# A two-block transformer on one core: the key bias traced into the first feed-forward product with loads on GpSimd's queue, position terms into the first attention, two modulation sums into the second attention

## The chip, the core and the metric

One NeuronCore of a Trainium2 chip runs the whole program. Its engines are TensorE (PE in the profile; PEld is its weight load), VectorE (DVE), ScalarE (ACT), GpSimd (POOL) and SyncE (SP, which only issues transfers here). Each works through its own instructions in order and waits for the others on semaphores. The metric is device time in microseconds, lower is better.

## The reference, cut to what matters

Two transformer blocks follow one another on x of shape 1 x 256 x 1024. The first has sparse attention with a gated MLP beside it and a SwiGLU network; the second is modulated by six rows computed from a vector c, and mixes latent attention with a state-space scan. The change touches the modulation and the position bias of the second block:

```python
mod = (jax.nn.silu(c) @ ada_w + ada_b)[:, None, :]
shift_m, scale_m, gate_m, shift_f, scale_f, gate_f = jnp.split(mod, 6, axis=-1)
...
h = rmsnorm(x, pre_norm_mix) * (1.0 + scale_m) + shift_m
proj = h @ w_in                                # q_lat, kv_lat, k_idx, w_idx, z, ...
...
bias = rel_bias[t5_bucket_2(pos_sel - pos_b[..., None])]
logits = jnp.einsum('bqhc,bqkc->bhqk', q_b, kv_sel) * scale + jnp.transpose(bias, (0, 3, 1, 2))
...
h2 = rmsnorm(x, pre_norm_ffn) * (1.0 + scale_f) + shift_f
```

`ada_w` is 1024 x 6144; row j of the modulation is columns j*1024 to (j+1)*1024 (0 shift_m, 1 scale_m, 2 gate_m, 3 shift_f, 4 scale_f, 5 gate_f). Rows 1 and 0 are needed at the end of the first block, 2 after the second block's mixer, 4 and 3 after that, 5 last.

## The kernel before

**Products.** The 256 tokens are two tiles of 128 (t0, t1). Each product is exact to fp32 by three matmuls: a weight tile `raw` of 512 KB is loaded by SP (`wload`, a ring of NRAW = 6 buffers), ACT casts it to `hi` (L266), DVE subtracts to `lo` (L267; a ring of four of each), and PE multiplies hi, lo and hi again with the two parts of the input (L274 to 276, columns up to 512; L351 to 353 with 256). So a load, a cast, a subtraction and twelve or more matmuls follow each other for every tile, and DVE's place in its own queue decides when PE gets a `lo`.

**Stages.** In the profiled execution: the first attention to about 127 us, its output product w_out to 150, the first feed-forward network (f1) to 362, of which the product with w_down is 280 to 362; then the latent projection `lat` (496 columns), `zproj` (the first four pairs of columns of z) and the key bias, to 435; the second attention to 570, its output product w_o_attn to 583; then the state-space part, its output products and the second feed-forward network to the end. `weave` interleaves generators by shares when it traces; after that a scheduler orders each engine by the order of tracing as priority and by its own model of when things are ready.

**Modulation sums.** `ada(j)` (L497 on) loads eight tiles `araw` of 512 KB on SP's queue, each multiplied by a column of silu(c) and added up on DVE (L504 for the first, L506 for seven), sums over partitions by four small matmuls (L518) and writes row j to DRAM. Its `araw` ring has two buffers of its own. The sums 1, 0, 2, 4, 3 are woven into f1, sum 5 into the second feed-forward network.

**Position terms and key bias.** `pos_prep` (L864 to L903, with loads on ACT's queue) turns the positions into clipped distances `rel_dr` in DRAM, and cuts the bias table into bf16 parts; it is traced at the start of f1, so its operations stand in w_out and f1. `key_bias` (L906 on) makes the bias of all 16 heads for 256 x 256 pairs. In eight steps it loads a tile `rb` of 512 KB from `rel_dr` (L914, SP's queue, two buffers; the source is four rows of keys, each spread over 32 partitions), clips it to the limits of the partition's bucket into `oh` (L917, one buffer), compares (L918, `is_equal`, back into rb), and then twice runs a burst of 24 small matmuls (L924) with an ACT copy into `kb` (L926). After every fourth step two tiles kb of 1 MB go to DRAM (L929); the second attention reads them as `bq`. Two steps' loads are placed by the scheduler in f1, the rest stands around `lat`: eight parts of the key bias are traced ahead of the first token tile of `lat`, two ahead of the second (KBN).

Of the kernel before, what the change touches and what calls it, by code (L numbers as in the profile page):

```python
# [20 lines left out]
P = 128  # L21
# [16 lines left out]
# how far one product runs ahead of its neighbour, and the shares in which interleaved parts are traced  # L38
KBN = (8, 2)
# [6 lines left out]
SCHED = {"a1": (2.0, 1.08), "f1": (3.0, 2.4), "f1ada": (1, 0, 2, 4, 3), "a2": (2.0, 0.63), "f2": (3.0, 1.45),  # L46
# [43 lines left out]
def body(tc, I, O):  # L90
# [91 lines left out]
    # ---------------------------------------------------------------- inputs that come first  # L182
# [27 lines left out]
    # ---------------------------------------------------------------- helpers  # L210
# [15 lines left out]
    def rstd2(a, b, n, eps):  # L226
        """(sum of squares + n*eps)**-0.5: the reciprocal norm over sqrt(n)"""
# [58 lines left out]
    def proj(W, c0, n, KT, xT, evac, extra=None, sizes=(2,), bank=ma, pre=None):  # L286
        """token-major product with columns c0..c0+n; evac(t, psum)"""
# [27 lines left out]
    def proj2(W, KT, xT, evac, order=None, sizes=(2,), tail=4):  # L315
        """token-major product with 1024 columns; xT(k) or a pair gives the stationary tiles"""
# [18 lines left out]
    def projT(W, c0, n, KT, xT, evac, bank=None, wide=True):  # L335
        """feature-major product; evac(first 128-column tile, psum of two tiles)"""
# [21 lines left out]
    def residual(t, accs, prow32, grow, shift, xT, want_r):  # L358
        """x += norm(mix) * gain, then the next norm's transposed input; its scale is left out when want_r"""
# [125 lines left out]
    # ---------------------------------------------------------------- modulation rows of the second block  # L485
# [12 lines left out]
    def ada(j, pl, bufs=2):  # L498
        acc = T(per, [P, 1024], tag="ada", bufs=1)
        for k in range(8):  # L500
            raw = wload(ktile(I["ada_w_2"], k, 1, j * D, D), (1, 1024), tag="araw", bufs=bufs, pl=pl)[:, 0]
# [29 lines left out]
    # ---------------------------------------------------------------- first block  # L531
# [17 lines left out]
    def first_rstd(t):  # L549
# [5 lines left out]
        r1[t] = rr  # L555

    with pool("a1") as ap, pool("a1w") as aw:
# [272 lines left out]
        with queued():  # L830
# [5 lines left out]
            conditioning()  # L836
            ck = compress(0, I["cmp_pos_k"][0], I["cmp_w1_k"][0], I["cmp_w2_k"][0])
# [586 lines left out]
```

## Time and profile before

| | us |
|---|---|
| three runs | 1040.60, 1036.82, 1041.38 |
| their median | 1040.6 |
| span of the profiled execution | 1032.4 |
| PE busy in it | 943.0 (91%) |
| DVE busy in it | 734.4 (71%) |
| ACT busy in it | 508.2 (49%) |

The profile is one execution on the chip. Its span runs from the first to the last instruction; a run's time has a few microseconds more around that. A page gives busy times and the chain of work that ended last; the other views used are a table of stretches, the waits of an engine, the chain piece by piece, and the instructions of one tile or line.

### The profile page before, as it was taken

Reading aid. Unit: us, or ns where it says so; the run is one execution under the profiler, and the core shown is the slowest. Engines: PE = TensorE matmul, PEld = TensorE weight load, DVE = VectorE, ACT = ScalarE, POOL = GpSimd, SP = SyncE. Lnnn points to the kernel's source line nnn. Section 1 sums busy time; section 2 is a strip of 40 time slices with the busy share of each in tenths; the row PEclk is TensorE's granted clock in tenths of the full one; section 3 lists DMA queues with packets and bytes.
Section 4 is the critical chain, followed back from the end, with each engine's and each line's share of the span. In section 5 each row is a group of like instructions: output and inputs, shape, how many; then the busy total and the mean of one; then the engine's idle time right before and its main releaser. Section 6 shows DMA issues by size and latency. Waiting matters only on the chain.

```text
span 1032.4 us, 15890 instructions
## 1 busy us (share of the span) xinstructions
PE 943.0 (91%) x6029; PEld 797.7 (77%) x6029; DVE 734.4 (71%) x1317; ACT 508.2 (49%) x873; POOL 20.5 (2%) x38
## 2 busy tenths in 40 slices
PE   7989999799999876799999949999999979999997
PEld 5766667589988655787786738889967859999885
DVE  6648788588887664489987546988897676565544
ACT  5427554334444342376576415876764454444442
POOL 1000000000000001000000000000000000000000
PEclk9999999989999988899999978999999989999999
DMA  8871358887888846666643359959666626666651
GB/s 285 256 268 42 123 183 263 247 268 231 295 289 305 268 118 191 187 175 175 192 129 97 123 153 237 225 136 229 159 192 206 204 84 203 192 191 219 185 184 41
DMA packets 158640, 200.02 MB, mean 194 GB/s; under 512 B 15564, under 2 KB 120293, under 8 KB 158565
## 3 DMA queue, kind: packets, MB, share of 16 engines
q1 hardware_dynamic: 137696, 184.61, 59.3%
q10 hardware_dynamic: 20868, 14.41, 4.7%
q8 instruction: 47, 0.77, 0.3%
q14 instruction: 29, 0.23, 0.1%
HBM read 193.45 MB, written 5.54 MB: 193 GB/s over the span
## 4 chain that ended last, share of the span: by engine, by line
PE 59%; DMA 19%; DVE 14%; issue 3%; ACT 3%; POOL 1%; SPq 0%; ACTq 0%; DVEq 0%; POOLq 0%
PE ma L275 6%; PE ma L274 6%; PE ma L276 6%; DVE lo L267 4%; PE ma L353 4%; DMA rb<-t 4%; PE ma L351 4%; PE ma L352 4%; PE mb L351 4%; PE mb L352 3%; PE mb L353 3%; PE mb L276 3%; PE mb L274 3%; PE mb L275 3%; DMA araw<-in_ada_w_dram 3%
## 5 line engine op out<-in xcount | busy, mean ns | idle before, releaser
L266 ACT CAST hi<-raw 128x1024 fp32r<-128x1024 f32 (+2 forms) x266 | 275.4, 1042 | 235.9 <-PE mb L276 79.5
L267 DVE TENSOR_TENSOR lo<-raw,hi 128x1024 fp32r<-128x1024 f32 (+2 forms) x266 | 319.9, 1212 | 90.7 <-ACT hi L266 88.8
L353 PE MATMUL ma<-xTh,lo 128*128 128x256 f32 x512 | 147.3, 288 | 0.9 <-DVE lo L267 0.8
L351 PE MATMUL ma<-xTh,hi 128*128 128x256 f32 x512 | 147.3, 288 | 0.0
L352 PE MATMUL ma<-xTl,hi 128*128 128x256 f32 x512 | 147.0, 287 | 0.0
L353 PE MATMUL mb<-xTh,lo 128*128 128x256 f32 x384 | 108.0, 281 | 0.5 <-DVE lo L267 0.5
L351 PE MATMUL mb<-xTh,hi 128*128 128x256 f32 x384 | 108.0, 281 | 0.0
L352 PE MATMUL mb<-xTl,hi 128*128 128x256 f32 x384 | 107.8, 281 | 0.0
L353 PEld LDWEIGHTS ma<-xTh,lo 128*128 128x128 f32 x512 | 98.7, 193 | 3.8 <-DVE lo L267 1.9
L351 PEld LDWEIGHTS ma<-xTh,hi 128*128 128x128 f32 x512 | 98.7, 193 | 1.2 <-issue 0.7
L352 PEld LDWEIGHTS ma<-xTl,hi 128*128 128x128 f32 x512 | 98.6, 193 | 1.1 <-issue 0.8
L274 PE MATMUL ma<-hi,xTh 128*128 128x512 f32 (+2 forms) x208 | 86.9, 419 | 12.8 <-ACT row L970 12.6
L275 PE MATMUL ma<-lo,xTh 128*128 128x512 f32 (+2 forms) x208 | 85.7, 414 | 7.1 <-DVE lo L267 7.1
L276 PE MATMUL ma<-hi,xTl 128*128 128x512 f32 (+2 forms) x208 | 84.5, 409 | 0.1
L353 PEld LDWEIGHTS mb<-xTh,lo 128*128 128x128 f32 x384 | 72.3, 188 | 1.3 <-DVE lo L267 0.7
L351 PEld LDWEIGHTS mb<-xTh,hi 128*128 128x128 f32 x384 | 72.3, 188 | 0.4 <-issue 0.4
L352 PEld LDWEIGHTS mb<-xTl,hi 128*128 128x128 f32 x384 | 72.3, 188 | 0.2 <-issue 0.2
L506 DVE SCALAR_TENSOR_TENSOR ada<-araw,t,ada 128x1024 f32<-128x1024 f32 x42 | 53.8, 1281 | 22.3 <-DMA araw<-in_ada_w_dram 22.1
L274 PEld LDWEIGHTS ma<-hi,xTh 128*128 128x128 f32 x208 | 41.7, 201 | 24.5 <-ACT row L970 13.0
L275 PEld LDWEIGHTS ma<-lo,xTh 128*128 128x128 f32 x208 | 41.6, 200 | 18.8 <-DVE lo L267 10.0
L276 PEld LDWEIGHTS ma<-hi,xTl 128*128 128x128 f32 x208 | 41.5, 199 | 9.5 <-issue 0.9
L275 PE MATMUL ma<-lo,hTh 128*128 128x512 f32 x88 | 35.0, 398 | 3.2 <-DVE lo L267 3.2
(411 smaller groups left out, 1769.4 us busy)
## 6 DMA issues: line engine op xcount, KB each, us to landing
raw<-in_w_in_dram SPq DMA_DIRECT2D x80, 512.0 KB
araw<-in_ada_w_dram SPq DMA_DIRECT2D x48, 512.0 KB
raw<-in_w_gate_up_dram SPq DMA_DIRECT2D x44, 512.0 KB
raw<-in_w_ffn_in_dram SPq DMA_DIRECT2D x44, 512.0 KB
raw<-in_w_down_dram SPq DMA_DIRECT2D x22, 512.0 KB
raw<-in_w_ffn_out_dram SPq DMA_DIRECT2D x22, 512.0 KB
raw<-in_w_out_dram SPq DMA_DIRECT2D x16, 512.0 KB
raw<-in_w_o_ssd_dram SPq DMA_DIRECT2D x16, 512.0 KB
```

The costliest lines, as they stand in the source:

```text
L266: s.copy(hi, raw)
L267: v.tensor_tensor(lo, raw, hi.bitcast(F32), op=OP.subtract)
L274: pe.matmul(out, xh, wh, start=start, stop=False)
L275: pe.matmul(out, xh, wl, start=False, stop=False)
L276: pe.matmul(out, xl, wh, start=False, stop=stop)
L351: pe.matmul(out, hi[:, k % pc, fs], xh[:, k], start=k == 0, stop=False)
L352: pe.matmul(out, hi[:, k % pc, fs], xl[:, k], start=False, stop=False)
L353: pe.matmul(out, lo[:, k % pc, fs], xh[:, k], start=False, stop=k == KT - 1)
L506: v.scalar_tensor_tensor(acc, raw, cc, acc, op0=OP.mult, op1=OP.add)
```

## The change

`pos_prep` and its tiles move from the start of f1 into the first attention, behind `conditioning()`. `key_bias` is traced inside f1, between the modulation sums 0 and 2, and its loads go to GpSimd's queue (`g.dma_start`) instead of SP's. `lat` then runs alone. The sums 4 and 3 leave f1 and are woven into the second attention, with a share of 0.4 of the second part's; there they use the common `raw` ring of six instead of a ring of their own. Comments and docstrings are also taken out, which shifts line numbers: L267 becomes L266, the rb load L914 becomes L615, its clip and comparison L618 and L619, the bursts L625.

```diff
-SCHED = {"a1": (2.0, 1.08), "f1": (3.0, 2.4), "f1ada": (1, 0, 2, 4, 3), "a2": (2.0, 0.63), "f2": (3.0, 1.45),
+SCHED = {"a1": (2.0, 1.08), "f1": (3.0, 2.4), "a2": (2.0, 0.63), "f2": (3.0, 1.45),
...
-    def ada(j, pl, bufs=2):
+    def ada(j, pl=None):
         acc = T(per, [P, 1024], tag="ada", bufs=1)
+        own = dict(tag="araw", bufs=2, pl=pl) if pl else {}
         for k in range(8):
-            raw = wload(ktile(I["ada_w_2"], k, 1, j * D, D), (1, 1024), tag="araw", bufs=bufs, pl=pl)[:, 0]
+            raw = wload(ktile(I["ada_w_2"], k, 1, j * D, D), (1, 1024), **own)[:, 0]
...
+    ppg = pool("pp", side="right")
+    pp = ppg.__enter__()
...
-                sy.dma_start(rb, bass.AP(tensor=rd.tensor, offset=rd.offset + (k * P + kk * 4) * S,
-                                         ap=[[8 * S, 4], [0, 32], [1, 8 * S]]))
+                g.dma_start(rb, bass.AP(tensor=rd.tensor, offset=rd.offset + (k * P + kk * 4) * S,
+                                        ap=[[8 * S, 4], [0, 32], [1, 8 * S]]))
...
             conditioning()
+            pos_prep()
...
-    pos_prep()
     wa, wd = SCHED["f1"]
     weave((ffn(xT, I["w_gate_up"][0], I["w_down"][0], rf, ev_f1), wa),
-          (seq(*(ada(j, rp) for j in SCHED["f1ada"])), wd))
+          (seq(ada(1, rp), ada(0, rp), key_bias(), ada(2, rp)), wd))
+    rpg.__exit__(None, None, None)
+    ppg.__exit__(None, None, None)
...
-    lat = proj(W, 0, 496, 8, xT, ev_lat, extra=[(0, 0, 464), (464, 6608, 32)], sizes=(4,))
-    for n in KBN:
-        steps_of(kbg, n)
-        steps_of(lat, 1)
-    run(lat)
-    run(kbg)
-    rpg.__exit__(None, None, None)
+    run(proj(W, 0, 496, 8, xT, ev_lat, extra=[(0, 0, 464), (464, 6608, 32)], sizes=(4,)))
...
-    weave((seq(indexer(), latent_v(), heads()), wa), (seq(zproj(NZ0, NZ - NZ0), *gproj, ssd_in(0, ap)), wf))
+    weave((seq(indexer(), latent_v(), heads()), wa), (seq(zproj(NZ0, NZ - NZ0), *gproj, ssd_in(0, ap)), wf),
+          (seq(ada(4), ada(3)), wf * 0.4))
```

How the scheduled order changes is shown at three places of DVE's queue. The numbers in names are buffers and differ between the kernels.

The end of w_out in the kernel before (`lo` are its last four splits, `pi` parts of the positions):

```order
L864 TENSOR_SCALAR pi_1507<-pi_1505 128x256
L865 CAST t_1496<-pi_1507 128x256
L867 TENSOR_SCALAR pi_1510<-pi_1505 128x256
L504 TENSOR_SCALAR ada_1610<-araw_1611,t_86 128x1024
L267 TENSOR_TENSOR lo_1334<-raw_1331,hi_1333 128x1024
L267 TENSOR_TENSOR lo_1340<-raw_1337,hi_1339 128x1024
L868 CAST t_1496<-pi_1510 128x256
L267 TENSOR_TENSOR lo_1346<-raw_1343,hi_1345 128x1024
L267 TENSOR_TENSOR lo_1352<-raw_1349,hi_1351 128x1024
```

The same place after the change:

```order
L266 TENSOR_TENSOR lo_1389<-raw_1386,hi_1388 128x1024
L266 TENSOR_TENSOR lo_1395<-raw_1392,hi_1394 128x1024
L504 TENSOR_SCALAR ada_1613<-araw_1614,t_86 128x1024
L618 TENSOR_SCALAR oh_2583<-rb_540_2581,t_79 128x2048
L266 TENSOR_TENSOR lo_1401<-raw_1398,hi_1400 128x1024
L266 TENSOR_TENSOR lo_1407<-raw_1404,hi_1406 128x1024
L506 SCALAR_TENSOR_TENSOR ada_1613<-araw_1641,t_86,ada_1613 128x1024
L619 TENSOR_TENSOR rb_540_2581<-oh_2583,rb_540_2581 128x2048
```

An rb load's clip `oh` now stands ahead of the last two splits of w_out, and the positions' operations are gone from there.

In the product with w_down before, splits alternate with the last operations of a modulation sum:

```order
L267 TENSOR_TENSOR lo_3110<-raw_3107,hi_3109 128x1024
L267 TENSOR_TENSOR lo_3116<-raw_3113,hi_3115 128x1024
L506 SCALAR_TENSOR_TENSOR ada_3046<-araw_3131,t_86,ada_3046 128x1024
L506 SCALAR_TENSOR_TENSOR ada_3046<-araw_3170,t_86,ada_3046 128x1024
L267 TENSOR_TENSOR lo_3149<-raw_3146,hi_3148 128x1024
L267 TENSOR_TENSOR lo_3155<-raw_3152,hi_3154 128x1024
L506 SCALAR_TENSOR_TENSOR ada_3046<-araw_3185,t_86,ada_3046 128x1024
L506 SCALAR_TENSOR_TENSOR ada_3046<-araw_3212,t_86,ada_3046 128x1024
```

After the change, splits alternate with the key bias:

```order
L266 TENSOR_TENSOR lo_3294<-raw_3291,hi_3293 128x1024
L618 TENSOR_SCALAR oh_3319<-rb_633_3317,t_79 128x2048
L266 TENSOR_TENSOR lo_3300<-raw_3297,hi_3299 128x1024
L619 TENSOR_TENSOR rb_633_3317<-oh_3319,rb_633_3317 128x2048
L266 TENSOR_TENSOR lo_3337<-raw_3334,hi_3336 128x1024
L618 TENSOR_SCALAR oh_3448<-rb_649_3446,t_79 128x2048
L619 TENSOR_TENSOR rb_649_3446<-oh_3448,rb_649_3446 128x2048
L266 TENSOR_TENSOR lo_3343<-raw_3340,hi_3342 128x1024
```

The sums are gone from there, and `oh` of the fifth and of the sixth rb load each stand ahead of a split.

The end of the second attention before (L1142 scales a head's weights, `mTl` is the second part of a head's output, `lo` are the splits of w_o_attn; four more stand further up among the heads):

```order
L1142 TENSOR_SCALAR L_5712<-L_5712,dn_5714 128x256
L1139 RECIPROCAL dn_5734<-dn_5734 128x2
L1142 TENSOR_SCALAR L_5732<-L_5732,dn_5734 128x256 x2
L234 TENSOR_TENSOR mTl_4903<-mb_5751,mTh_4902 128x256
L267 TENSOR_TENSOR lo_5837<-raw_5834,hi_5836 128x1024
L267 TENSOR_TENSOR lo_5843<-raw_5840,hi_5842 128x1024
L267 TENSOR_TENSOR lo_5849<-raw_5846,hi_5848 128x1024
L267 TENSOR_TENSOR lo_5855<-raw_5852,hi_5854 128x1024
L1185 SCALAR_TENSOR_TENSOR t_3519<-t_3519,ma_5758 128x512
L1185 SCALAR_TENSOR_TENSOR t_3519<-t_3519,ma_5759 128x512
```

After the change (L1146 is the same scaling):

```order
L1146 TENSOR_SCALAR L_5684<-L_5684,dn_5686 128x256 x2
L506 SCALAR_TENSOR_TENSOR ada_5728<-raw_5732,t_86,ada_5728 128x1024
L506 SCALAR_TENSOR_TENSOR ada_5728<-raw_5735,t_86,ada_5728 128x1024
L233 TENSOR_TENSOR mTl_4849<-mb_5703,mTh_4848 128x256
L506 SCALAR_TENSOR_TENSOR ada_5728<-raw_5738,t_86,ada_5728 128x1024
L506 SCALAR_TENSOR_TENSOR ada_5728<-raw_5741,t_86,ada_5728 128x1024
L506 SCALAR_TENSOR_TENSOR ada_5728<-raw_5744,t_86,ada_5728 128x1024
L506 SCALAR_TENSOR_TENSOR ada_5728<-raw_5747,t_86,ada_5728 128x1024
L266 TENSOR_TENSOR lo_5769<-raw_5766,hi_5768 128x1024
L506 SCALAR_TENSOR_TENSOR ada_5728<-raw_5750,t_86,ada_5728 128x1024
L266 TENSOR_TENSOR lo_5775<-raw_5772,hi_5774 128x1024
L519 TENSOR_TENSOR scr_5753<-at_5755,scr_5753 128x256
```

Operations of sum 3 now stand between the last head and the splits of w_o_attn, none of which is left among the heads.

## Rows read from the trace of the kernel before

**Rows 1.** Page: an engine's busy us, share and instructions; the chain by engine.

```profile
PE 943.0 (91%) x6029; PEld 797.7 (77%) x6029; DVE 734.4 (71%) x1317; ACT 508.2 (49%) x873; POOL 20.5 (2%) x38
...
PE 59%; DMA 19%; DVE 14%; issue 3%; ACT 3%; POOL 1%; SPq 0%; ACTq 0%; DVEq 0%; POOLq 0%
```

**Rows 2.** Stretches: length, busy us (instructions) per engine, PE clock, DMA share, GB/s.

```profile
200.00:215.00 15.00, 7.62 (x35) 6.50 (x34) 6.71 (x8) 2.67 (x3) 0.00 (x0) 0.66 0.71 237
240.00:280.00 40.00, 39.96 (x340) 39.20 (x339) 31.24 (x37) 18.55 (x21) 0.00 (x0) 1.00 0.81 257
280.00:345.00 65.00, 64.95 (x353) 54.81 (x352) 51.96 (x53) 26.26 (x28) 0.00 (x0) 1.00 0.87 299
345.00:365.00 20.00, 15.89 (x92) 12.04 (x91) 15.79 (x22) 8.04 (x17) 1.09 (x2) 0.91 0.71 208
362.00:435.00 73.00, 50.85 (x570) 45.15 (x570) 37.54 (x64) 25.15 (x56) 6.04 (x8) 0.81 0.58 158
435.00:530.00 95.00, 91.84 (x592) 78.05 (x591) 86.84 (x209) 61.16 (x114) 0.00 (x0) 1.00 0.62 182
530.00:570.00 40.00, 39.17 (x233) 29.63 (x232) 29.83 (x88) 25.65 (x65) 0.00 (x0) 1.00 0.32 96
```

**Rows 3.** Chain of work, 120 to 210 us: start, duration, engine or load.

```profile
128.70 3.17 DMA pi<-in_positions_dram
131.90 0.30 DVE pi L864
...
170.95 16.90 DMA rb<-t
```

**Rows 4.** The same chain, 325 to 440 us.

```profile
343.88 4.81 DMA raw<-in_w_in_dram
...
350.55 0.43 PE ma L276
...
353.89 0.23 PE ma L275
...
355.83 0.70 ACT junk L223 x2
...
361.85 0.66 PE tr L245 x4
362.50 0.23 PE mb L276
...
363.74 0.81 PE at L924 x24
...
366.94 11.42 DMA rb<-t
...
390.17 18.74 DMA t<-kb
...
414.91 9.65 DMA rb<-t
```

**Rows 5.** Line L353, 362 to 440 us: duration ns (min/median/max), first and last start.

```profile
L353 PE MATMUL mb<-qnh,lo x8: 276/281/281, 434.2 to 439.8; 128*128 128x256 f32 x8
```

**Rows 6.** Waits of PE, 150 to 362 us: total us, times, longest.

```profile
PE tr L245 <- DVE scr L420: 7.5, 2, 7.3
```

**Rows 7.** Loads issued from 270 to 345 us.

```profile
araw<-in_ada_w_dram SPq DMA_DIRECT2D x16, 512.0 KB
```

**Rows 8.** Chain of work, 0 to 60 us.

```profile
29.98 8.54 DMA t<-t
```

**Rows 9.** Tile rb (duration ns) and page (split `lo`: busy, mean ns).

```profile
L917 DVE TENSOR_SCALAR oh<-rb,t x8: 811/812/816, 187.9 to 424.7; 128x2048 bf16<-128x2048 bf16 x8
L918 DVE TENSOR_TENSOR rb<-oh,rb x8: 1212/1217/1226, 190.9 to 425.9; 128x2048 bf16<-128x2048 bf16 x8
...
L267 DVE TENSOR_TENSOR lo<-raw,hi 128x1024 fp32r<-128x1024 f32 (+2 forms) x266 | 319.9, 1212 | 90.7 <-ACT hi L266 88.8
```

**Rows 10.** Line L506, the whole span: duration ns.

```profile
L506 DVE SCALAR_TENSOR_TENSOR ada<-araw,t,ada x42: 1275/1283/1286, 138.5 to 785.3; 128x1024 f32<-128x1024 f32 x42
```

More of the change, by code (lines that the diff above doesn't have):

```diff
@@ L37 @@
 NSCR = 3
-KBN = (8, 2)
 NZ = 8
@@ new lines, in body, with pos_prep @@
+    pmat = T(per, [P, 3, S])
+    pcol = T(per, [P, 3, 2])
+    relc = T(pp, [P, 2, S], BF)
+    rel_dr = T(dr, [S, S], BF)
+    tp = T(pp, [P, 3, 64], BF)
+    def pos_prep():
+        pr = T(pp, [P, S], I32, tag="pi", bufs=2)
+        s.dma_start(pr, bass.AP(tensor=pos.tensor, offset=pos.offset, ap=[[0, P], [1, S]]))
+        pos_parts(pmat[:, 0], pmat[:, 1], pmat[:, 2], pr)
+        pc = T(pp, [P, 2], I32)
+        s.dma_start(pc, pos.rearrange("o (a p) -> p (o a)", p=P))
+        pos_parts(pcol[:, 0], pcol[:, 1], pcol[:, 2], pc)
+        tb = T(pp, [P, 4, 16])
+        g.memset(tb, 0.0)
+        for i in range(4):
+            s.dma_start(tb[i * 32:(i + 1) * 32, i, :], I["rel_bias_2"])
+        tbf = tb.rearrange("p a h -> p (a h)")
+        v.tensor_scalar(tp[:, 0], tbf, -1.0, None, op0=OP.mult)
+        rem = T(pp, [P, 64])
+        v.scalar_tensor_tensor(rem, tbf, -1.0, tp[:, 0], op0=OP.mult, op1=OP.subtract)
+        v.tensor_copy(tp[:, 1], rem)
+        v.tensor_tensor(tp[:, 2], rem, tp[:, 1], op=OP.subtract)
+        for k in range(2):
+            a = T(pp, [P, S], tag="ra", bufs=1)
+            b_ = T(pp, [P, S], tag="rb", bufs=1)
+            v.tensor_scalar(a, pmat[:, 0], pcol[:, 0, k:k + 1], -4096.0, op0=OP.subtract, op1=OP.mult)
+            v.tensor_scalar(b_, pmat[:, 1], pcol[:, 1, k:k + 1], -1.0, op0=OP.subtract, op1=OP.mult)
+            v.tensor_tensor(a, a, b_, op=OP.add)
+            v.tensor_scalar(relc[:, k], a, 120.0, -120.0, op0=OP.min, op1=OP.max)
+        s.dma_start(rel_dr[:, :].rearrange("(k p) q -> p k q", p=P), relc)
@@ new lines, in body, with key_bias @@
+    bias_dr = T(dr, [2, P, 16, S])
+    def key_bias():
+        for k in range(2):
+            dst = [T(rp, [P, 16, P], tag="kb", bufs=2) for _ in range(2)]
+            for kk in range(0, 32, 8):
+                rb = T(rp, [P, 8, S], BF, tag="rb8", bufs=2)
+                rd = rel_dr[:, :]
+                g.dma_start(rb, bass.AP(tensor=rd.tensor, offset=rd.offset + (k * P + kk * 4) * S,
+                                        ap=[[8 * S, 4], [0, 32], [1, 8 * S]]))
+                oh = T(rp, [P, 8, S], BF, tag="oh", bufs=1)
+                v.tensor_scalar(oh, rb, bkt[:, 0:1], bkt[:, 1:2], op0=OP.max, op1=OP.min)
+                v.tensor_tensor(rb, oh, rb, op=OP.is_equal)
+                yield
+                for t in range(2):
+                    b = atb()
+                    for i in range(8):
+                        for j in range(3):
+                            pe.matmul(b[:, i * 64:(i + 1) * 64], rb[:, i, t * P:(t + 1) * P], tp[:, j], start=j == 0,
+                                      stop=j == 2)
+                    s.copy(dst[t][:, :, kk * 4:kk * 4 + 32].rearrange("p h (i j) -> p h i j", i=4),
+                           b.rearrange("p (j i h) -> p h i j", h=16, i=4))
+                    if kk == 24:
+                        s.dma_start(bias_dr[t, :, :, k * P:(k + 1) * P], dst[t])
+                    yield
@@ L1154, in heads @@
                 split_ps(oT, mT[0][:, h4 // 2 + pr], mT[1][:, h4 // 2 + pr])
-    kbg = key_bias()
-    next(kbg)
     def steps_of(gen, n):
```

76 lines of the change are left out of this document (12 added, 64 removed).

## The prediction

> **What bounds the kernel now.** I read the page first: PE is busy for 943.0 of 1032.4 us, yet only 59% of the chain that ended last is PE; 19% is DMA [rows 1]. So the kernel is PE-bound except in a few places where a load holds everything. The table of stretches finds them [rows 2]: from 240 to 345 us PE is busy without a gap, from 362 to 435 us only 50.85 of 73 us, at a granted clock of 0.81, and from 200 to 215 us 7.62 of 15 us at 0.66. The chain names the loads: rb at 170.95 (16.90 us), 366.94 (11.42) and 414.91 (9.65), between the last two the 18.74 us write of kb, and a raw load at 343.88 [rows 3, 4]. A stall costs twice, since the first products after it run slower: 0.43 us each at 350.55, 0.23 at 353.89 [rows 4].
>
> **The change, part by part.** The profiled execution has a span of 1032.4 us, the three runs a median of 1040.6; I count differences in the profile and subtract them from the median.
>
> *The latent stage, freed of key bias: -43 us.* The last down product of the second token tile ends at 362.5, the indexer's first query product starts at 434.2 [rows 4, 5]: about 72 us. What must lie between without key bias: the residual's vector chain, 6.0 us for the other tile (355.83 to 361.85) [rows 4]; transposes and splits, 2.5; the latent product of the second tile, 24 matmuls at 0.23 = 5.5, of which I count a part at the slow clock, +2.5; zproj's 96 matmuls at 39.96/340 = 0.1175 us [rows 2] = 11.3, under which the query norm's chain hides; the three bursts of key bias that order still leaves behind the end, 3 x 0.81 [rows 4], fit into the 6.0. Together 28 to 29 us, so 43 are saved; 38 if zproj waits for a split or two, 46 at full clock. What is late next there is PE itself.
>
> *The stall at 200 us: -10.* DVE's in-order queue sat on the second rb load and the transposes behind it waited 7.3 us [rows 6]; in the table 7.4 us are idle and a third of the 7.6 busy us is lost to the clock [rows 2]. In the new order both early rb loads are issued in w_out, the second one's use is some 180 PE products later: the stall goes.
>
> *The raw stall at 345 us: -5.* PE idles 4.1 of 20 us at clock 0.91 [rows 2], where 16 modulation loads share SP's queue with the weights [rows 7]. These leave; 0 to -6.
>
> *Position terms in the first attention: +3 (0 to +7).* Not free: on ACT's queue three position loads now stand ahead of the 1 MB table load whose 8.54 us are on the chain at 29.98 [rows 8], and about 20 DVE operations of 0.3 us [rows 3] stand ahead of the copies and splits behind it. In w_out they leave the chain, but one `is_equal` (1.22 us) and one wait come instead.
>
> *First rb load in w_out: +4 (-1 to +10).* It can only be issued after the last attention transposes; DVE meets its `oh` ahead of the last two splits of w_out, and PE has 36 products, 36 x 0.23 = 8.3 us, until it needs the first of them. Landing takes L, then `oh` 0.81 and a split 1.21 us [rows 9]. With L = 10 this is 12.0 against 8.3. Before, DVE waited at that place for the 3.17 us load of the positions [rows 3], which stalled PE by less than 1 us.
>
> *Key-bias products in f1: +10.* 13 of 16 bursts of 24 move under a PE that has no gap [rows 2], 13 x 0.81 [rows 4].
>
> *Six rb loads in the down product: +21 (1 to 62).* This decides. Each load waits for the last product that reads the tile two before it (two buffers), and DVE meets its `oh` before a split that PE needs. Counting products of 0.23 us (0.1175 in gate/up) and bursts between the two in the order gives PE's cover: 11.5, 10.7, 11.5, 7.4, 12.9 and 7.9 us for loads three to eight. From landing to the split's end are 2.03 us where only `oh` stands ahead, 3.25 where `is_equal` does too [rows 9] (third, sixth, seventh, eighth). At L = 10 the stalls are 1.8, 1.3, 0.5, 5.9, 0.4 and 5.4 = 15 us, and two are long enough for the clock to fall, 2.7 us each as after the stall at 200 us: +21. No load on GpSimd's queue is in this trace, so L is bounded: 4.81, what a raw load of the same 512 KB takes [rows 4], gives 1; 16.90, the rb load beside the gate/up loads [rows 3], gives 57, or 62 with the clock. I take 10, near the two of the latent stage (11.42 and 9.65): with 16 modulation loads gone [rows 7] the 22 weight loads of 512 KB and rb ask for some 15 MB in 85 us, 175 GB/s, less than the 299 of before and close to the 158 of that stage [rows 2].
>
> That rb takes twice a raw load's time points to few DMA engines at work on it. The Trainium skill (DMA: Bandwidth & Descriptors, section Why a DMA increments its semaphore by 16 and not by 1) says that a transfer uses the largest number up to 16 that divides the slowest dimension on both sides; here that is 4, which agrees with 9.65 against 4.81, and by it the queue makes no difference: +21 stays.
>
> *Modulation sums 4 and 3 in the second attention: +14 (+4 to +25).* Sixteen DVE operations, two of them shorter, the others 1.28 us [rows 10]. By the order eight meet the stretch 435 to 530, where DVE is busy 86.84 and PE 91.84 of 95 us [rows 2]: 10 us into 8.2 of slack, so 2 to 10; I take 5. The other eight come with the last heads, seven of them between the last head's scaling and the first split of w_o_attn; all 96 products of w_o_attn now stand behind the heads, where a third stood among them. 7 x 1.28 + 1.2 = 10.2 us, less 3 of head work still on PE: 7 idle, 2.7 of clock, +9 or so. The 33 products taken from among the heads leave there what they add behind, as PE is busy 39.17 of 40 us [rows 2].
>
> Sum: -43 - 10 - 5 + 3 + 4 + 10 + 21 + 14 = -6, a span of about 1026 and a time of **1035 us**. Its own range is 1022 to 1049.
>
> **The rivals.**
>
> *rb lands as fast as a raw load.* For it: the raw load's 4.81 us for as many bytes [rows 4], and a queue of its own need not wait behind SP's weights. Against: all rb rows of before are slow. With L = 5 to 7 the stalls are 1 to 6 us and w_out's goes: 1035 - 20 = **1015**.
> The page named above gives the mechanism as an exception: on trn2 a load from GpSimd's queue sometimes takes 16 engines whatever the outer dimension. No run so far shows it.
>
> *rb lands late, slower than before.* One mechanism: the load competes with the weight stream, as the one of 170.95 did (16.90). Each microsecond of L above 10 costs six in the down product and one in w_out, so near L = 11 the gain of 6 is gone, and at 14 to 16.9 the time is 1035 + 28 to 48; I take **1066**. For it: the down product wants weights throughout, and two 1 MB kb writes lie in it, 18.74 us each before [rows 4], with ACT's next kb copy and the casts behind it waiting for them. Against: less traffic than before.
> A second rule of the Trainium skill speaks against the move (SBUF — State Buffer, section SBUF: two separate sides): GpSimd writes such a load's descriptors itself and is locked out while DVE runs a fast-mode operation. The trace of before has no such load; the operation it could wait for lasts 0.81 us here [rows 9], so by it the sum would be worse by under 6 us, which I leave out.
>
> *The modulation sums stay wholly on the path.* Their loads now share SP's queue and the six raw buffers with weights, bq and w_o_attn, so a late sum holds the next weight. Then 10 + 16 us: 1035 + 12 = **1047**. For it: DVE's 91% there. Against: the DMA share of 0.32 from 530 to 570 [rows 2].
>
> **How the numbers follow.** Chances: forecast 0.40, fast rb 0.27, late rb 0.17, modulation 0.16. About 0.5%, 5 us, is what a measurement can tell, so faster means below 1035.4 and slower above 1045.8. The forecast's range gives faster 0.20, same 0.17, slower 0.03; the fast rival all faster; the late one all slower; modulation same 0.05, slower 0.11. Sum: faster 0.47, same 0.22, slower 0.31. The range runs from 1007, the fast rival with the latent stage at its best, to 1060, which leaves out the worse half of the late one and little else. Both signs stay open, since a term of 43 us stands against four unknown ones.
>
> **What would show it.** The stretch from the end of down to the first query product should be near 29 us instead of 72; no PE gap some 60 us into f1; in the down product the waits of DVE's `oh` for rb, longest for the sixth and eighth load. If these are short, the fast rival; if all six exceed 14 us from issue, the late one. In the second attention PE should idle 5 to 9 us between the last head and w_o_attn. The prediction is wrong as a whole if zproj or the query norm in the freed stage waits for weights, or if GpSimd's issue itself takes microseconds.

## The result: 0.9% slower, where 0.5% faster was forecast

| | before | after |
|---|---|---|
| median of eight runs each, us | 1036.57 | 1046.63 |
| lowest and highest, us | 1031.59, 1042.99 | 1041.76, 1051.37 |
| span of the profiled execution, us | 1032.4 | 1040.5 |

The ratio is 1.0089, with a 95% interval of 1.006 to 1.0119. The forecast was 1035, its range 1007 to 1060; the measured time lies inside the range, but on the other side of the kernel before. A run more than 1.5% above the fastest of its kernel is left out of the medians and ratios below. Per stage, from the two profiled executions (a stage ends where the last product named ends):

| stretch | before, us | after, us | forecast | measured |
|---|---|---|---|---|
| start to the last down product of f1 | 362.7 | 383.2 | +23 | +20.5 |
| from there to the first query product (the latent stage) | 71.3 | 44.4 | -43 | -26.9 |
| second attention with w_o_attn | 150.4 | 169.9 | +14 | +19.5 |
| the rest | 448.0 | 443.0 | 0 | -5.0 |
| span | 1032.4 | 1040.5 | -6 | +8.1 |

So the stages that should have become longer did, by about what was said. The stage that should have paid for them gave 16 us less.

The page of after, as in [rows 1]: busy times, the queue that GpSimd issues to (packets, MB, share), the chain.

```profile
PE 942.8 (91%) x6029; PEld 793.0 (76%) x6029; DVE 734.4 (71%) x1317; ACT 510.0 (49%) x873; POOL 25.5 (2%) x46
...
q0 software_dynamic: 4224, 4.21, 1.4%
...
PE 56%; DMA 15%; issue 14%; DVE 10%; ACT 3%; POOL 1%; SPq 0%; DVEq 0%; ACTq 0%; POOLq 0%
```

PE does the same work; DMA's share of the chain fell from 19% to 15%, PE's from 59% to 56%; "issue", the time in which an engine waited for nothing that the profile shows, rose from 3% to 14%. Stretches of after, columns as in [rows 2]:

```profile
200.00:215.00 15.00, 15.00 (x138) 14.56 (x137) 13.36 (x16) 6.27 (x7) 0.00 (x0) 1.00 1.01 353
...
280.00:292.50 12.50, 8.58 (x70) 8.54 (x71) 10.66 (x12) 4.76 (x6) 0.00 (x0) 0.73 0.41 131
292.50:383.20 90.70, 76.79 (x548) 60.03 (x545) 41.54 (x47) 32.91 (x46) 4.48 (x7) 0.94 0.60 173
383.20:427.60 44.40, 30.95 (x219) 25.52 (x215) 26.42 (x53) 17.95 (x40) 4.38 (x8) 0.88 0.67 191
427.60:597.50 169.90, 154.35 (x913) 124.42 (x913) 140.73 (x322) 92.57 (x183) 0.00 (x0) 0.97 0.58 179
```

The stall at 200 us is gone: 15.00 of 15 us busy at full clock, 7.62 at 0.66 before. In its place PE idles 3.9 us from 280 to 292.5 and 13.9 us in the product with w_down, 90.7 us long instead of 68.2 (its first product starts at 292.5 us here and at 294.5 before, not at 280 as the stages above have it). The latent stage holds 30.95 us of PE work in 44.40. Who waits for the rb loads (tile rb; total us, times), and how long each takes from issue:

```profile
  DMA rb<-t: 42.4, 7
...
DMA to landing us min/median/max: 8.1/10.7/14.1
```

DVE stood 42.4 us at `oh`, and PE behind it. PE's waits in the rest of f1, from 155 to 292.5 and from there to 383.2 us (total, times, longest):

```profile
PE mb L352 <- DVE lo L266: 6.2, 1, 6.2
```

```profile
PE ma L274 <- DVE lo L266: 12.9, 6, 3.2
```

The latent stage: first the longest loads of the chain, then DVE's and PE's waits.

```profile
384.02 6.26 DMA scr<-in_ada_b_dram
...
395.71 3.55 DMA scr<-in_post_norm_mix_dram
...
404.42 5.79 DMA raw<-in_ada_w_dram
```

```profile
DVE scr L519 <- DMA scr<-in_ada_b_dram: 2.5, 1, 2.5
DVE scr L522 <- DMA scr<-in_post_norm_mix_dram: 2.2, 1, 2.2
...
DVE ada L504 <- DMA raw<-in_ada_w_dram: 0.9, 1, 0.9
```

```profile
PE tr L1048 <- DVE scr L1043: 6.5, 2, 5.5
PE ma L274 <- DVE lo L266: 6.2, 2, 4.9
```

None of the three loads is the stage's own: the first two finish sum 2 (its bias row and the norm's weights, L519 and L522), the third opens sum 4. Each stands in DVE's queue ahead of a split or a norm that PE needs.

### The profile page after: what moved, and what is told of

It is laid out like the page before. It is cut to its first block, busy times and chain, and to the rows that moved or that the text cites. A ratio compares the mean times of both kernels' runs of the same rounds, so it can differ in the third digit from the quotient of the medians.

```text
span 1040.5 us, 15910 instructions
## 1 busy us (share of the span) xinstructions
PE 942.8 (91%) x6029; PEld 793.0 (76%) x6029; DVE 734.4 (71%) x1317; ACT 510.0 (49%) x873; POOL 25.5 (2%) x46
## 3 DMA queue, kind: packets, MB, share of 16 engines
q0 software_dynamic: 4224, 4.21, 1.4%
## 4 chain that ended last, share of the span: by engine, by line
PE 56%; DMA 15%; issue 14%; DVE 10%; ACT 3%; POOL 1%; SPq 0%; DVEq 0%; ACTq 0%; POOLq 0%
PE ma L274 5%; PE ma L275 5%; PE ma L273 5%; DMA rb<-t 4%; PE ma L351 3%; PE mb L350 3%; PE ma L350 3%; PE ma L352 3%; PE mb L352 3%; PE mb L351 3%; PE mb L273 3%; PE mb L275 3%; PE mb L274 3%; DVE lo L266 2%; DMA t<-in_d_skip_dram 2%
## 5 line engine op out<-in xcount | busy, mean ns | idle before, releaser
L266 DVE TENSOR_TENSOR lo<-raw,hi 128x1024 fp32r<-128x1024 f32 (+2 forms) x266 | 320.3, 1213 | 110.3 <-ACT hi L265 108.1
L351 PE MATMUL ma<-xTl,hi 128*128 128x256 f32 x512 | 144.3, 282 | 0.0
L273 PE MATMUL ma<-hi,xTh 128*128 128x512 f32 (+2 forms) x208 | 85.3, 413 | 13.0 <-ACT row L974 12.7
L274 PE MATMUL ma<-lo,hTh 128*128 128x512 f32 x88 | 36.7, 417 | 12.9 <-DVE lo L266 12.9
L506 DVE SCALAR_TENSOR_TENSOR ada<-araw,t,ada 128x1024 f32<-128x1024 f32 x28 | 35.9, 1282 | 7.2 <-DMA araw<-in_ada_w_dram 7.1
```

The lines of the kernel that those rows point to most:

```text
L266: v.tensor_tensor(lo, raw, hi.bitcast(F32), op=OP.subtract)
L273: pe.matmul(out, xh, wh, start=start, stop=False)
L274: pe.matmul(out, xh, wl, start=False, stop=False)
L351: pe.matmul(out, hi[:, k % pc, fs], xl[:, k], start=False, stop=False)
L506: v.scalar_tensor_tensor(acc, raw, cc, acc, op0=OP.mult, op1=OP.add)
```

## Experiments

The theory after the result: the key bias in f1 costs what its loads' 10 us cost, the freed stage doesn't shrink to 28.5 us because foreign work lies in it, and the sums in the second attention cost more than 14 us. Rivals: GpSimd's queue makes the loads slow; the sums are cheap and the stalls in f1 are all of it; the 28.5 us were wrong in themselves. Every ratio is to the kernel before on the same chip. Every kernel's engine orders are set anew by the scheduler, so an edit can also move operations that it doesn't name; stage lengths are from one profiled execution each.

### The queue: rb loads back on SP's

```diff
-                g.dma_start(rb, bass.AP(tensor=rd.tensor, offset=rd.offset + (k * P + kk * 4) * S,
-                                        ap=[[8 * S, 4], [0, 32], [1, 8 * S]]))
+                sy.dma_start(rb, bass.AP(tensor=rd.tensor, offset=rd.offset + (k * P + kk * 4) * S,
+                                         ap=[[8 * S, 4], [0, 32], [1, 8 * S]]))
```

> The changed kernel with the eight rb loads on SP's queue again, all else as changed. Theory A (how long an rb load takes has nothing to do with the queue, the losses come from where it stands): issue to landing stays at 9 to 14 us, and the time within 8 us of the changed kernel's 1046.6, rather above it, since weight loads now queue behind an rb issue that waits for PE. Theory B (GpSimd's queue is what makes the loads late): landing in 5 to 8 us and a time of 1025 to 1035.

Measured: 1052.05 us, ratio 1.0156 [1.0111, 1.0202]; waits at `oh`:

```profile
  DMA rb<-t: 51.2, 6
```

DVE waits 9 us longer than with GpSimd's queue and the kernel takes 5 us more, where the two intervals just touch. So the new queue seems to help rather than harm, and it isn't why DVE waits for the loads; their landings on SP's queue are not in the trace.

### The sums 4 and 3 back in f1

```diff
-          (seq(ada(1, rp), ada(0, rp), key_bias(), ada(2, rp)), wd))
+          (seq(ada(1, rp), ada(0, rp), key_bias(), ada(2, rp), ada(4, rp), ada(3, rp)), wd))
...
-          (seq(ada(4), ada(3)), wf * 0.4))
```

> The changed kernel with the modulation sums 4 and 3 back in f1, behind sum 2, with their own two buffers; the second attention is woven of two parts as before. Theory A (the sums cost the second attention and w_o_attn about 10 us, by the trace from 445.2 to 597.1 against 442.6 to 584.0): 10 us faster there, but some of it given back in the product with w_down, where 16 tiles more are loaded beside rb: 1036 to 1045. Rival (the loss to w_o_attn has another cause): no gain between the latent stage and the end of w_o_attn, time 1046 or above.

Measured: 1056.34 us, ratio 1.0182 [1.0139, 1.0225]. The latent stage and the second attention with w_o_attn:

```profile
392.80:457.60 64.80, 37.12 (x235) 29.04 (x232) 44.83 (x71) 17.86 (x40) 7.10 (x8) 0.76 0.79 242
457.60:606.50 148.90, 145.83 (x889) 119.79 (x889) 122.40 (x304) 91.25 (x183) 0.00 (x0) 1.00 0.50 149
```

Without the two sums the second attention takes 148.9 us, less than before (150.4) and 21 less than after: there the sums cost 20 us. But f1 has no room for them behind the key bias; they ran into the latent stage, which grew by 20.4 us, while f1 grew by 9.6. The time is above the 1036 to 1045 expected.

### Sum 2 ahead of the key bias

```diff
-          (seq(ada(1, rp), ada(0, rp), key_bias(), ada(2, rp)), wd))
+          (seq(ada(1, rp), ada(0, rp), ada(2, rp), key_bias()), wd))
```

> The changed kernel with the key bias traced behind sum 2 instead of ahead of it. Theory A (in the latent stage DVE sat 2.5 and 2.2 us on the two small loads with which sum 2 ends, PE 4.9 and 1.3 us behind it, at the slow clock afterwards): these waits are gone, the stage from the last down product to the first query product falls from 44.6 to about 37 us; if the key bias moves back by as much as sum 2 moves ahead, more of its bursts fall behind the end of f1, some 2 to 6 us. Time 1036 to 1046. Rival (the stage is bound by the norm chain of the query whatever stands in DVE's queue): the stage stays above 42 us, time 1046 or more.

Measured: 1043.71 us, ratio 1.0045 [1.0011, 1.0079]. Sum 2's loads are gone from the latent stage, but now the key bias's end lies in it: from 374.4 us the stage takes 50.2 us, not the 37 hoped for. Two pieces of the chain, one in f1 and one in the stage:

```profile
354.21 11.28 DMA rb<-t
...
376.55 13.11 DMA rb<-t
```

With loads of 11 to 13 us, in each of these orders something falls out of f1. The next experiments make the loads shorter.

### The same bytes in four loads

```diff
-                g.dma_start(rb, bass.AP(tensor=rd.tensor, offset=rd.offset + (k * P + kk * 4) * S,
-                                        ap=[[8 * S, 4], [0, 32], [1, 8 * S]]))
+                for c in range(4):
+                    g.dma_start(rb[c * 32:(c + 1) * 32],
+                                bass.AP(tensor=rd.tensor, offset=rd.offset + (k * P + kk * 4 + 8 * c) * S,
+                                        ap=[[0, 32], [1, 8 * S]]))
```

> The changed kernel with each rb load issued as four loads of 32 partitions, one for each row of keys, still on GpSimd's queue. Theory A (an rb load is slow because its outer dimension of four lets few DMA engines work on it): landing falls from 10.7 to 5 to 7 us, the stalls of PE in f1 (some 24 us by the trace) fall to under 6, time 1024 to 1034. Rival B (the queue or the traffic makes it slow): landing stays at 9 us or more, with four issues instead of one rather longer, time 1044 to 1056.

Measured: 1016.27 us, ratio 0.9798 [0.9765, 0.9831], 30 us less than after. Queue, waits at `oh`, and landing:

```profile
q0 software_dynamic: 1536, 4.20, 1.7%
```

```profile
  DMA rb<-t: 10.8, 5
...
DMA to landing us min/median/max: 2.8/5.3/8.2
```

These landings are of quarters. The third tile's four, by their line from 264 to 268 us:

```profile
L616 POOL DMA_DIRECT2D rb<-t x4: 489/489/544, 264.9 to 266.4; - x4
...
DMA to landing us min/median/max: 5.1/7.2/7.4
```

So this tile is complete 8.9 us after its first issue. Over the eight tiles the median is 8.4 us (4.7 to 9.5), against 10.7 (8.1 to 14.1) for one load; that makes 26 us less in all. DVE's wait falls from 42.4 to 10.8 us, and w_down's product takes 71.5 us instead of 90.7. The same four loads on SP's queue:

```diff
-                    g.dma_start(rb[c * 32:(c + 1) * 32],
+                    sy.dma_start(rb[c * 32:(c + 1) * 32],
```

> The changed kernel with the four-part rb loads on SP's queue instead of GpSimd's. Theory A (the queue matters little): landing 5 to 8 us, time 1013 to 1024, rather above 1016.3, as rb issues that wait for PE hold weight loads back. Theory B (GpSimd's queue is what lets the short loads through beside the weights): landing over 8 us, time above 1026.

Measured: 1023.36 us (three of four runs), ratio 0.9873 [0.9814, 0.9933]. The trace has landings for five of the 32 quarters, with a median of 5.4 us, and DVE waits 8.9 us at `oh`, so the loads are no later on SP's queue. The kernel is 7 us slower than on GpSimd's queue; the intervals again overlap at their ends, the first clip stands at 170.2 us instead of 138.7, and what makes the difference is not shown. Two loads of 64 partitions each, with an outer dimension of two:

```diff
-                g.dma_start(rb, bass.AP(tensor=rd.tensor, offset=rd.offset + (k * P + kk * 4) * S,
-                                        ap=[[8 * S, 4], [0, 32], [1, 8 * S]]))
+                for c in range(2):
+                    g.dma_start(rb[c * 64:(c + 1) * 64],
+                                bass.AP(tensor=rd.tensor, offset=rd.offset + (k * P + kk * 4 + 16 * c) * S,
+                                        ap=[[8 * S, 2], [0, 32], [1, 8 * S]]))
```

> The changed kernel with each rb load issued as two loads of 64 partitions, two rows of keys each, on GpSimd's queue. Theory A (the number of DMA engines that work on a load follows from its outer dimension, four engines for one load of four rows, two for each load of two): two loads together still have four engines, landing stays at 8.5 to 12 us and the span within 8 us of the changed kernel's 1040.5. Rival (several loads in flight are what helps, whatever their shape): landing 6 to 8 us, span 1022 to 1032.

Measured: 1051.24 us in one run. Queue, and landing of a half:

```profile
q0 software_dynamic: 8448, 4.22, 1.8%
```

```profile
DMA to landing us min/median/max: 9.6/13.0/18.5
```

More loads alone don't help: a tile is now complete after 13.9 us at the median, more than the 8.5 to 12 expected. The shape decides. The Trainium skill (DMA: Bandwidth & Descriptors, section Why a DMA increments its semaphore by 16 and not by 1) has a transfer use the largest number of engines up to 16 that divides that dimension: four for one load, two for each half, sixteen for 32 partitions. The order of the tiles' times, 10.7, 13.9 and 8.4 us, agrees, and so do the packets. The data go in 1024 packets of 4096 bytes in all three forms, so it isn't their size; the others have 4 bytes. Without 16 per load, the data are 128 of 512 packets of one load, 64 of 512 of a half and all 32 of a quarter: 4, 2 and 16 sixteenths. The Trainium skill's exception on the same page, sixteen engines for some loads from GpSimd's queue, is not seen.

### Four loads in the kernel before

Only the load of before is changed, on SP's queue, and nothing else is edited:

```diff
-                sy.dma_start(rb, bass.AP(tensor=rd.tensor, offset=rd.offset + (k * P + kk * 4) * S,
-                                         ap=[[8 * S, 4], [0, 32], [1, 8 * S]]))
+                for c in range(4):
+                    sy.dma_start(rb[c * 32:(c + 1) * 32],
+                                bass.AP(tensor=rd.tensor, offset=rd.offset + (k * P + kk * 4 + 8 * c) * S,
+                                        ap=[[0, 32], [1, 8 * S]]))
```

> The kernel before with nothing changed but each rb load issued as four loads of 32 partitions on SP's queue. Theory A (slow rb loads are what holds the latent stage of before and stalls f1 at 200 us): landing 5 to 7 us instead of 9 to 17, the stall at 200 us goes (10 us) and about half of the latent stage's idle time, time 1010 to 1020; then moving the key bias under f1 is worth little beyond it. Theory C (the move itself is worth something once loads are fast): this kernel gains less, 1020 to 1030, and stays above the changed kernel with split loads, 1016.3.

Measured: 1010.43 us, ratio 0.9751 [0.9688, 0.9814]. The stretch of the old stall, the latent stage with all of the key bias in it, and the clips:

```profile
200.00:215.00 15.00, 15.00 (x117) 14.26 (x115) 12.82 (x15) 6.33 (x7) 0.00 (x0) 1.00 0.94 295
...
353.20:407.20 54.00, 41.24 (x557) 36.68 (x557) 35.09 (x63) 23.47 (x54) 6.96 (x8) 0.91 0.53 148
```

```profile
L919 DVE TENSOR_SCALAR oh<-rb,t x8: 802/807/815, 231.0 to 403.4; 128x2048 bf16<-128x2048 bf16 x8
```

The latent stage falls from 71.3 to 54.0, and DVE waits 4.0 us at `oh` in all, 30.0 before. The stall at 200 us is gone, but that is not shown to come from short loads: the first tile's quarters are issued between 172.2 and 216.4 us, and the scheduler put its clip at 231.0 us instead of 187.9 [rows 9]. The second attention takes 159.9 us, 9.5 more than before, which was not followed. The whole change with four loads (1016.27) is no better than four loads without it (1010.43). The same on GpSimd's queue:

```diff
-                    sy.dma_start(rb[c * 32:(c + 1) * 32],
+                    g.dma_start(rb[c * 32:(c + 1) * 32],
```

> The kernel before with split rb loads on GpSimd's queue. Theory A (with short loads GpSimd's queue is worth some us, as 1016.3 against 1024.2 in the changed kernel, since SP's weight loads no longer queue behind an rb issue that waits): 1002 to 1009 against 1010.4 on SP's queue. Rival (no difference where the key bias stands around the latent product): 1009 to 1014.

Measured: 1026.0 us, ratio 0.9912 [0.9877, 0.9947], not the 1002 to 1009 expected. The scheduler, told of another queue, set another order: f1 is 9 us longer and bursts of the key bias slid into the second attention. The loads weren't it (waits at `oh` 1.2 us in all); which part of the order did it is left open.

### What keeps the freed stage long

First sum 2, moved to the second attention (with the slow loads of after):

```diff
-          (seq(ada(1, rp), ada(0, rp), key_bias(), ada(2, rp)), wd))
+          (seq(ada(1, rp), ada(0, rp), key_bias()), wd))
...
-          (seq(ada(4), ada(3)), wf * 0.4))
+          (seq(ada(2), ada(4), ada(3)), wf * 0.4))
```

> The changed kernel, slow rb loads and all, with sum 2 woven into the second attention ahead of sums 4 and 3 instead of f1. Theory A (sum 2's two late loads cost the latent stage 6 to 8 us): DVE no longer waits on scr there, the stage from the last down product to the first query product falls from 44.6 to 36 to 40 us; eight more operations in the second attention cost 8 to 12 us there. Time 1044 to 1054. Rival (the stage's length is set by the query's norm chain): stage above 43 us, time 1054 or more.

Measured: 1056.2 us, ratio 1.0192 [1.0143, 1.0241]. The latent stage takes 38.7 us instead of 44.4, so sum 2's end costs 5.7 there. The second attention takes 180.0 instead of 169.9: a third sum in it, ten more. F1 takes 7.2 us more, though a sum left it, and the time is above the 1044 to 1054 expected.

Then the change with four loads, and sum 2 ahead of the key bias in f1:

```diff
-          (seq(ada(1, rp), ada(0, rp), key_bias(), ada(2, rp)), wd))
+          (seq(ada(1, rp), ada(0, rp), ada(2, rp), key_bias()), wd))
```

> The changed kernel with split rb loads on GpSimd's queue and sum 2 traced ahead of the key bias. Theory A (behind the fast loads, what is left in the latent stage is the end of sum 2: 2.5 and 2.2 us of DVE, 5 to 7 us of PE with the clock): from the end of the first tile's down products to the first query product 56 us fall to 46 to 50, time 1006 to 1013. Rival (the norm chain of the query binds the stage): stage stays above 53 us, time 1014 to 1020.

Measured: 1014.82 us, ratio 0.9791 [0.9735, 0.9847], a latent stage of 52.3 us with the last bursts inside; 1006 to 1013 had been expected. With a larger share for the woven part nearly all of them end in time; this kernel is the base of all that follow:

```diff
-SCHED = {"a1": (2.0, 1.08), "f1": (3.0, 2.4),
+SCHED = {"a1": (2.0, 1.08), "f1": (3.0, 3.0),
```

> The changed kernel with split rb loads, sum 2 ahead of the key bias, and the share of the second part of f1's weave 3.0 instead of 2.4, so that by the order sum 2 and all bursts of the key bias end inside f1. Theory A (the predicted 28.5 us of the latent stage are right once nothing else stands in it): from the last down product to the first query product 28 to 36 us, time 1000 to 1009. Rival (28.5 us was wrong in itself, since DVE's and PE's own order of the norm chain and zproj takes longer): 38 us or more, time 1009 to 1016.

Measured: 1011.47 us, ratio 0.976 [0.9713, 0.9807]. Sum 2 is gone from the stage, and of the key bias only the last 41 small matmuls (1.4 us) are left; its stretch, PE's waits in it, and the first of zproj's three kinds of product:

```profile
357.90:396.90 39.00, 30.18 (x211) 25.88 (x207) 25.51 (x50) 18.01 (x40) 4.38 (x8) 0.87 0.74 211
```

```profile
PE tr L1050 <- DVE scr L1045: 5.3, 2, 4.6
PE ma L274 <- DVE lo L266: 2.7, 1, 2.7
```

```profile
L350 PE MATMUL ma<-xTh,hi x32: 277/282/562, 381.6 to 396.1; 128*128 128x256 f32 x32
```

39.0, not 28.5: the estimate was wrong in itself. PE waits for the norm chain (L1045), which I had put under zproj. Two suspects follow. Sum 4's first operation, with its load, stands in that chain; here the two sums begin three steps later (`idle(n)`, a new generator, yields n times):

```diff
-          (seq(ada(4), ada(3)), wf * 0.4))
+          (seq(idle(3), ada(4), ada(3)), wf * 0.4))
```

> As the run with share 3.0, with sums 4 and 3 beginning three steps later in the weave of the second attention, so that no operation of theirs stands among the query's norm chain. Theory A (the first operation of sum 4 waits for its tile in that chain and PE waits behind it, 2 to 4 us): stage 2 to 4 us shorter than in that run, and the same amount lost later at most in part; time 0 to 4 us less. Rival (PE waits there for the chain in any case): stage equal within 1 us, time equal within 3 us.

Measured: 1015.84 us, ratio 0.9802 [0.9749, 0.9856], the two profiled spans 1008.6 and 1010.0: no difference that can be told. The stage is 36.6, so 2.4 shorter; the second attention gives it back (172.7 for 168.6).

The other suspect: zproj adds up in `ma`, the pair of PSUM banks that holds the latent product until DVE's last copy from it, so its first product can't start before the first token tile's norm chain is done (in the kernel above DVE's last copy of that tile from `ma` starts at 381.2 us, zproj at 381.6). Here its first part uses `mb`:

```diff
-    run(zproj(0, NZ0))
+    run(projT(W, 464, NZ0 * P, 8, xT, ev_z(0), mb, wide=False))
```

> As e12_rows_share3, but zproj in the freed stage sums up in the pair of banks called mb instead of ma. Theory A (in e12 zproj could not start until DVE had taken the last part of the latent product out of ma, so 96 products of 0.12 us stood behind the norm chain instead of under it): the first zproj product starts while the norm chain runs, the stage from the end of down to the first query product falls from 39.0 us to 33 to 35, time 1005 to 1010. Rival B (zproj waits for its weights or for the splits of them, or the query norm's own products then wait for mb): the stage stays at 37 us or more, time 1010 or more.

Measured: 1004.52 us, ratio 0.9686 [0.9647, 0.9724]. The stage, PE's waits and the first of zproj's three kinds of product:

```profile
358.00:390.90 32.90, 28.55 (x211) 24.54 (x208) 25.05 (x50) 17.82 (x40) 5.24 (x8) 0.95 0.88 252
```

```profile
PE ma L274 <- DVE lo L266: 2.7, 1, 2.7
PE tr L1050 <- DVE scr L1045: 1.6, 2, 0.8
```

```profile
L350 PE MATMUL mb<-xTh,hi x32: 277/280/363, 376.5 to 390.2; 128*128 128x256 f32 x32
```

zproj's first product starts 18.5 us into the stage instead of 23.7, the wait for the chain falls from 5.3 to 1.6 us, the granted clock rises from 0.87 to 0.95. The choice of banks is worth 6.1 us in the stage.

### What a sum costs in the second attention

Why two of them cost after 19.5 us is seen in PE's waits from 427.6 to 597.5 us, and in the chain at the end of the heads:

```profile
PE tr L1148 <- DVE L L1146: 5.5, 6, 1.9
PE ma L273 <- ACT hi L265: 5.1, 1, 5.1
```

```profile
567.08 4.68 DMA raw<-in_w_o_attn_dram
571.78 1.05 ACT hi L265
572.88 1.22 PE ma L273 x2
```

Before, L1144 (the same transposes) waited 1.3 us and w_o_attn not at all. The 5.1 us aren't DVE's adding: the first weight tile of w_o_attn was issued at 567.1, since sum 3's loads hold the six `raw` buffers and SP's queue. Twenty us there, from 557.6, have 12.7 busy. With only sum 3 there, and sum 4 in f1 ahead of the key bias:

```diff
-SCHED = {"a1": (2.0, 1.08), "f1": (3.0, 3.0),
+SCHED = {"a1": (2.0, 1.08), "f1": (3.0, 3.6),
...
-          (seq(ada(1, rp), ada(0, rp), ada(2, rp), key_bias()), wd))
+          (seq(ada(1, rp), ada(0, rp), ada(2, rp), ada(4, rp), key_bias()), wd))
...
-          (seq(ada(4), ada(3)), wf * 0.4))
+          (seq(ada(3)), wf * 0.4))
```

> As e12_rows_share3, but sum 4 stands in f1 again, ahead of the key bias, with f1's share at 3.6 so that the key bias still ends in time; only sum 3 is woven into the second attention. Theory A (each sum costs about 10 us in the second attention, where DVE is nearly as busy as PE, and little in f1): the stretch from the first query product to the end of w_o_attn falls from 168.6 us to 157 to 160, f1 and the freed stage change by less than 4 us, time 1001 to 1007. Rival B (f1 has no slack either once the key bias is in it, or its last bursts slip behind the down product): the 10 us come back there, time 1009 or more.

Measured: 1004.47 us, ratio 0.9678 [0.9626, 0.973]. The second attention with w_o_attn, and its first waits:

```profile
404.50:558.50 154.00, 147.39 (x897) 120.16 (x897) 130.15 (x312) 91.87 (x183) 0.00 (x0) 1.00 0.56 169
```

```profile
PE tr L1150 <- DVE L L1148: 2.1, 4, 0.8
PE at L1139 <- DVE mn L1141: 1.2, 1, 1.2
```

154.0 instead of 168.6 (the same kernel with both sums there, 1011.47 above): the first sum costs 154.0 - 150.4 = 3.6 us over before (5.1 over the 148.9 without a sum), the second 14.6. These prices hold for these orders: with no sum in it the stretch took from 148.9 to 159.9 us above. The wait for w_o_attn's weights is gone, the granted clock is 1.00 throughout. f1 is 8.1 us longer (366.0 for 357.9), more than the 4 that I had allowed, so the gain is about half of it. Both edits together:

```diff
-SCHED = {"a1": (2.0, 1.08), "f1": (3.0, 3.0),
+SCHED = {"a1": (2.0, 1.08), "f1": (3.0, 3.6),
...
-          (seq(ada(1, rp), ada(0, rp), ada(2, rp), key_bias()), wd))
+          (seq(ada(1, rp), ada(0, rp), ada(2, rp), ada(4, rp), key_bias()), wd))
...
-    run(zproj(0, NZ0))
+    run(projT(W, 464, NZ0 * P, 8, xT, ev_z(0), mb, wide=False))
...
-          (seq(ada(4), ada(3)), wf * 0.4))
+          (seq(ada(3)), wf * 0.4))
```

> Both edits, zproj in the other banks and sum 4 in f1. Theory A for both: the gains add, stage 33 to 35 us, second attention with w_o_attn 157 to 160, time 996 to 1003. If only one holds, the time of that one; 1009 or more if neither does.

Measured: 996.75 us, ratio 0.9621 [0.9567, 0.9674], three runs from 994.68 to 1002.95. The fourth, of 1009.94, is the profiled one, so its latent stage of 36.5 us, where 33 to 35 had been expected, can't be set against the others. The time is inside the expected 996 to 1003, and below every other kernel here; the interval overlaps those of the two single edits, so that the gains add is likely but not shown.

## Why the prediction was wrong, step by step

**Where it was right.** All that lies ahead of the end of f1 summed to +23 and measured +20.5. The position terms cost nothing in the first attention: w_out's first product starts at 117.5 us instead of 118.4, and the table load is still 8.18 us of the chain (8.54 in [rows 8]). The stall at 200 us went. The first load in w_out cost 2.5 us of PE from 120 to 150 us (27.05 busy of 30 us, 29.55 before) against +4. The loads' 10 us, taken from the latent stage's rows rather than from the 16.90 of [rows 3], measured 10.7 at the median, and PE's waits for splits 6.2 + 12.9 = 19.1 us against 15. That the sum came out so near is in part luck. For loads three to eight PE waited 6.2, 2.7, 3.2, 3.2, 3.0 and 0.6 us where 1.8, 1.3, 0.5, 5.9, 0.4 and 5.4 were counted, so the cover of single loads was wrong both ways; DVE's waits were shortest, not longest, for the sixth and eighth (3.6 and 3.5). And the clock fell to its lower level (0.50) four times there, from 282.4, 309.7, 337.0 and 360.9 us, not twice. "Fast rb" fell, with a shortest landing of 8.1; "late rb" fell too, with a longest of 14.1.

**The step that failed: the latent stage, -43 against -26.9.** It was mostly a sum of what PE has to do, and it put the wait for the query norm at nothing: "under which the query norm's chain hides". In its place PE waited 6.5 us there in after. Of 44.4 - 28.5 = 15.9 us the experiments show, one by one:

- Sum 2 ends there: 5.7 us, by moving it. I took the 16 modulation loads of [rows 7] as gone from f1's end and forgot that sum 2 is traced behind the key bias: its eight additions still run in f1, from 244.6 to 273 us, but its last steps come out behind the key bias.
- Sum 4's first operation sits in the norm's chain: 2.4 us, by starting it later.
- The norm's chain can't hide under zproj, as both use the banks `ma`: 6.1 us, by giving it the other pair.
- The remaining 1.7 us are not settled, and that the three sizes add is not shown, since each comes from another kernel. In the kernel with the share of 3.0, the one with the other banks and the two with a single sum, PE waits 2.7 to 3.7 us for a split of `lat`, which was to be ready by then.

The terms of the sum can be read off the kernel with the share of 3.0, 39.0 us long. The residual's chain took 7.6 us (357.9 to 365.5) for 6.0; in it stand the last bursts and products of the first token tile's `lat`, 24 that the sum doesn't name. Transposes took 2.0 for 2.5, the rest of `lat` 9.1 for 8.0. Then 5.0 us pass until zproj's first product, 4.6 of them waiting for the norm chain, counted at nothing. zproj takes 15.0 (381.6 to 396.6) for 11.3, as the chain's transposes stand among its products and the first ones run at the lower clock.

**The sums in the second attention, +14 against +19.5.** The place was right (heads, then the way to w_o_attn) and the rival had the better mechanism: loads on the common ring that hold the next weight. PE's idle time grew by 11.6 us (from 150.40 - 146.42 to 169.90 - 154.35), against 12 forecast. What was too small is the clock: PE's busy time grew by 7.9 us, of which 1.9 are the sums' own matmuls and 1.3 eight transposes that came earlier, so some 4.7 are left, put down to products at a lower clock (0.97 over the stretch, 1.00 before) by what remains; 2.7 had been counted. Some of it comes back: the rest of the program is 5.0 us shorter, as those transposes' wait further on fell from 2.9 to 0.7 us; the other part was not followed.

**What was not asked.** The prediction held the loads' length fixed and asked only which queue they stood on. Its own row, twice a raw load's time for the same bytes, named the cheaper edit: four loads in place of one make the kernel before 2.5% faster with nothing else edited, and a quarter of the latent stage goes. That edit also changed the scheduled order, so how much of the 2.5% is the shorter load alone is not shown; in the kernel after, where DVE's order stayed nearly the same, the loads gave 30 us.

## To carry to other kernels

Before moving a slow transfer under other work, ask why it is slow: cutting a broadcast source with an outer dimension of four into single rows gave more than every move tried here. When a stage is to shrink to its PE work, list who else shares its accumulators, its vector queue and its load ring; "hides under" holds only if the hidden work can start, and a fill-in product in the same PSUM banks as the stage's own result can't. Work pushed back in an interleaved sequence comes out at the stage's end, so price its last operations (small loads, waits, cross-engine steps) where they now land.

## What the hardware showed unexpectedly

- The same 512 KB from GpSimd's queue, from first issue to last landing: 10.7 us at the median as one load over four rows, 13.9 as two loads over two, 8.4 as four loads over one, with 4224, 8448 and 1536 packets for all eight, 1024 of them with data.
- On the queue itself: a quarter's landing of 5.3 us on GpSimd's and 5.4 on SP's, the latter from five loads only. The Trainium skill's rule that GpSimd is locked out of writing descriptors while DVE runs a fast-mode operation (SBUF — State Buffer, section SBUF: two separate sides) shows no price here; no run isolates it.
- The granted clock fell in the second attention of after to 0.91 from 507.6 to 547.6 us, where PE idled 2.6 of 40 us, behind 40 us with 4.1 idle. With one sum there (1004.47 us) the same stretch idled 1.9, behind 40 us with 4.0 idle, at a clock of 1.00. What decides between the two is not shown. L1156's products took 441 ns at the mean over the whole second attention, part of which ran at the lower clock, and 397 before (L1152).
